# Where the first projections accumulate, and over how many bank tags the second piece's transposes rotate, in a hybrid decoder layer

## The chip, the cores and the metric

The kernel runs on one core of a Trainium2 chip. A core has five engines that run side by side, each through its own list of instructions in order: TensorE (PE, matrix products), VectorE (DVE), ScalarE (ACT), GpSimd (POOL) and SyncE (SP, which issues most of the transfers). PE writes its results only to PSUM, the accumulator memory, which this kernel uses as eight banks. The metric is the device time of one execution in microseconds; less is better. The result is given as the median of several runs, and as a ratio to runs of the kernel before on the same chip.

## The reference

One layer with 1024 tokens plus 16 learned ones ahead of them, 1024 wide:

```python
u = rmsnorm(h, g_pre_mix[l])
z = u @ w_in[l]
q, k, v, xr, yr = jnp.split(z, split_at, axis=-1)
attn = sliding_window_attention_with_sinks(q, k, v, attn_sinks[l])   # window 128
xr = causal_depthwise_conv(xr, conv_w[l], conv_b[l])
hr = rg_lru(xr, w_a[l], b_a[l], w_x[l], b_x[l], lru_lambda[l])
rec = gelu(yr) * hr
mix = jnp.concatenate([attn, rec], axis=-1) @ w_out[l]
h = h + rmsnorm(mix, g_post_mix[l])
u = rmsnorm(h, g_pre_ffn[l])
f = jnp.square(jax.nn.relu(u @ w_ff1[l])) @ w_ff2[l]
h = h + rmsnorm(f, g_post_ffn[l])
```

The change touches only the first two lines: the normed rows `u` and their projections.

## The kernel before

Every product of 32-bit numbers is made of three matmuls. An operand is split into a high part (a rounded copy, made by ACT) and a low part (the rest, made by DVE), and high by high, high by low and low by high are summed in PSUM (`mm3`, L122 to L128; `split`, L93).

The opening stage takes the 1040 rows in four pieces (`ALL`, L243): 272 rows (the 16 learned ones among them), then three times 256. For each piece, in `transposed` (L284), PE turns the normed rows by transposes (L291), eight chunks of 128 columns, each chunk in a bank of its own; ACT (L116) and DVE (L117) then scale each chunk and write the high and the low part of `u`, which empties the bank. After that come four projections with 128 columns each: k, v, the first q and the first x. Every projection of a piece is 24 matmuls (8 chunks by three parts) into one bank, and a sink empties it:

- `sink_k` (L359, `put_k` L352) is a ladder: for each of two halves ACT copies (L355), DVE copies (L356), DVE subtracts (L357). In the first piece it is done twice, once for the 16 learned rows and once for the other 256.
- `sink_v` (L372) and `sink_x` (L390) are one copy by ACT each.
- `sink_q` (L379) is an ACT step (L116) and a DVE step (L117) for each of two halves.

The first piece is written out apart (L403 to L418): k and v in two banks, then q, then x, each part by part (`part`, L234). The later pieces use `project` (L220), whose matmuls are L124 to L126. The norms of the later pieces (L209, L215) are made on ACT, POOL and DVE; those of the third and fourth piece run while the second piece is at work.

PSUM has four tags of two banks: acc, s, pt and o (`bank`, L65). A request for a bank of a tag gets whichever of its two banks comes free first. In the first piece all four projections ask for acc. The transposes go round over pt, o and s (L288), six banks. Later in the kernel s is the tag of the attention scores.

The order of the instructions on each engine isn't the order of the text. A planner simulates the kernel and at each moment gives an engine the instruction that is ready and stands earliest in the text; the order that comes out is fixed in the program. An instruction that has no bank in the planner's time is passed over by others that have one. Some orders are tied by hand: `behind` (L105), and `chained` (L271), which keeps ACT's and DVE's work of the opening in a row. The transposes of the third piece are tied behind the last matmul of the first piece, and so on (`done`, L396). The remaining projections (fills, L641) carry a lower priority and go between the steps of the attention, from about 64 us on.

Of the kernel before, what the change touches and what calls it, by code (L numbers as in the profile page):

```python
# [37 lines left out]
def hybrid_layer(  # L38
# [26 lines left out]
    def bank(tag, shape=(P, 512)):  # L65
        uid[0] += 1
        return ps.tile(list(shape), F32, tag=tag, name=f"ps_{tag}{uid[0]}")
# [37 lines left out]
    def behind(name, *inss):  # L105
        for ins in inss:
            tc.add_manual_dep(
                ins, name,
                mybir.DependencyInfo(
                    mybir.DependencyClass.NoSync, mybir.DependencyReason.DATA  # L110
                ),
                reason="order",
            )

    def split_scaled(hi, lo, src, scale):
        high = nc.scalar.activation(hi, src, AF.Copy, scale=scale).ins  # L116
        low = nc.vector.scalar_tensor_tensor(  # L117
            lo, src, scale, f32(hi), op0=ALU.mult, op1=ALU.subtract
        ).ins
        return high, low  # L120
# [99 lines left out]
    def project(w, pieces, sink):  # L220
        wh, wl = w
        for t0, n in pieces:
            acc = bank("acc")
            for kc in range(KC):
                uh, ul = u[kc]
                mm3(
                    acc[:, :n], (wh[:, kc, :], wl[:, kc, :]),
                    (uh[:, t0 : t0 + n], ul[:, t0 : t0 + n]),
                    kc == 0, kc == KC - 1,
                )  # L230
            sink(acc[:, :n], t0, n)


    def part(acc, w, piece, k, last=2):  # L234
        t0, n = piece
        for kc in range(KC):
            last_mm[0] = nc.tensor.matmul(
                acc[:, :n], w[k // 2][:, kc, :], u[kc][k % 2][:, t0 : t0 + n],
                start=k == 0 and kc == 0, stop=k == last and kc == KC - 1,
                skip_group_check=True,  # L240
            ).ins.name
# [19 lines left out]
    flip = [0]  # L261

    def normed(b):
        rows = [(meta_t, NMETA)] if b == 0 else []
        rows += [(xt[2 * b], P), (xt[2 * b + 1], P)]
        return [(norm_rows(s[:m], m), m) for s, m in rows]
# [4 lines left out]
    def chained(e, ins):  # L271
        if last[e] is not None:
            behind(last[e], ins)
        last[e] = ins.name
# [9 lines left out]
    def transposed(b, xn, after=None):  # L284
        t0, n = ALL[b]
        for kc in range(KC):
            flip[0] += 1
            pt = bank(("pt", "o", "s")[flip[0] % 3])  # L288
            o = 0
            for s, m in xn:  # L290
                ins = nc.tensor.transpose(  # L291
                    pt[:, o : o + m], s[:m, kc * P : (kc + 1) * P], ident[:m, :m]
                )
                if after:
                    behind(after, ins.ins)
                o += m
            uh, ul = u[kc]
            high = split_scaled(
                uh[:, t0 : t0 + n], ul[:, t0 : t0 + n], pt[:, :n],
                g_mix_col[:, kc : kc + 1],  # L300
            )
            if b == 0:
                chained(0, high[0])
                chained(1, high[1])
# [24 lines left out]
    for i in range(4, 8):  # L329
        load_x(i)  # L330
    wk = high_w(rk, "b")
    transposed(0, xn)
    low_w(wk, rk)
    wv = high_w(rv, "b")
# [64 lines left out]
    for b in range(4):  # L399
        if b:  # L400
            transposed(b, xn if b == 1 else normed(b), done[b])
        piece = ALL[b]
        if b == 0:  # L403

            acc = [bank("acc"), bank("acc")]
            for a, w in zip(acc, (wk, wv)):
                part(a, w, piece, 0)
                part(a, w, piece, 1)
            for a, w, sink in zip(acc, (wk, wv), (sink_k, sink_v)):
                part(a, w, piece, 2)  # L410
                sink(a[:, : piece[1]], *piece)
            for w, (t0, n), sink in ((wq, (16, 256), sink_q0), (wx, piece, sink_x0)):
                acc = bank("acc")
                for k in range(3):
                    part(acc, w, (t0, n), k)
                sink(acc[:, :n], t0, n)
            done.append(last_mm[0])
            continue  # L418
        project(wk, [piece], sink_k)
        project(wv, [piece], sink_v)  # L420
        project(wq, [piece], sink_q0)
        project(wx, [piece], sink_x0)
        done.append(last_mm[0])
# [64 lines left out]
    for b in range(2):  # L488
        pv = bank("pt", (P, 4, P))
        for i in range(4):  # L490
            o = NMETA + (4 * b + i) * P
# [852 lines left out]
```

## Time and profile before

| | us |
|---|---|
| median of 3 runs | 986.53 |
| lowest and highest run | 982.86, 989.44 |
| profiled execution, first to last instruction | 984.1 |

The time of the profiled execution is its span. Busy time is given for each engine; a matmul's row has its start and its length to the end of its result, and matmuls overlap, so that the pace is read from the starts. In rows that end with a bracket, the bracket gives the idle time of the engine before them, and what ended it. In a table by stretches each engine has its busy time and, in brackets, its number of instructions, in the order PE, weight loads (PEld), DVE, ACT, POOL; then come PE's granted clock as a share of full speed, the busy share of the DMA engines and GB/s. Tiles are named by tag: ps_acc is a bank of acc, a is `u`, ws and b are weights and sinks' targets.

### The profile page before, as it was taken

To read this page: it belongs to the slowest core of one execution; us is meant where nothing else is said; L and a number is where in the kernel's file an instruction comes from. 1 tells how busy PE (TensorE), PEld (TensorE's weight loads), DVE (VectorE), ACT (ScalarE), POOL (GpSimd) and SP (SyncE) were. 2 spreads that over 40 slices of the span, in tenths; PEclk is the share of its full clock that TensorE was granted. 3 is DMA by queue.
4 is the path that set the end of the run, shared out by engine and by line. 5 is a ranking of instruction groups with operands and counts; after the bars stand their busy time and mean duration, and the time that the engine had idled before them with its cause. 6 is when DMAs were issued, how large, how long until landed. Compare 5 with 4: busy or idle time off the path is not lost.

```text
span 984.1 us, 12519 instructions
## 1 busy us (share of the span) xinstructions
PE 955.5 (97%) x4782; PEld 803.2 (82%) x4782; DVE 680.7 (69%) x1002; ACT 502.3 (51%) x809; POOL 71.9 (7%) x108
## 2 busy tenths in 40 slices
PE   6799999999999999999999999999999999999995
PEld 6798999889878887888888888888888788888874
DVE  6469997775885687665655465468567776779876
ACT  7356665457944554343555556654433343435331
POOL 4010000000002100000000000000111000002012
PEclk9799999999999999999999999999999999999998
DMA  8002100112134466576522364324678766647762
GB/s 282 23 12 63 25 23 22 43 44 65 65 129 147 149 216 193 173 256 200 197 96 86 97 202 130 106 88 122 167 182 190 182 224 190 193 152 191 226 182 85
DMA packets 89371, 133.28 MB, mean 135 GB/s; under 512 B 13752, under 2 KB 52680, under 8 KB 89312
## 3 DMA queue, kind: packets, MB, share of 16 engines
q1 hardware_dynamic: 81488, 112.04, 35.9%
q0 software_dynamic: 6960, 18.35, 8.8%
q10 hardware_dynamic: 864, 2.10, 0.6%
q8 instruction: 37, 0.61, 0.3%
q14 instruction: 22, 0.18, 0.1%
HBM read 113.60 MB, written 18.87 MB: 135 GB/s over the span
## 4 chain that ended last, share of the span: by engine, by line
PE 87%; DVE 5%; DMA 4%; ACT 2%; issue 1%; POOL 1%; POOLq 0%; SPq 0%; DVEq 0%; ACTq 0%
PE ps_acc L125 10%; PE ps_acc L124 10%; PE ps_acc L126 10%; PE ps_s L126 6%; PE ps_s L124 6%; PE ps_s L125 6%; PE ps_pt L124 6%; PE ps_pt L126 6%; PE ps_pt L125 6%; PE ps_o L125 5%; PE ps_o L124 5%; PE ps_o L126 5%; DMA raw<-in_w_ff_dram 2%; PE ps_o L577 2%; PE ps_pt L566 1%
## 5 line engine op out<-in xcount | busy, mean ns | idle before, releaser
L95 ACT CAST ws<-raw 128x1024 fp32r<-128x1024 f32 (+1 forms) x70 | 71.7, 1025 | 124.9 <-PE ps_o L125 47.7
L98 DVE TENSOR_TENSOR ws<-raw,ws 128x1024 fp32r<-128x1024 f32 (+1 forms) x71 | 84.7, 1194 | 54.7 <-ACT ws L95 54.5
L124 PE MATMUL ps_acc<-a,ws 128*128 128x256 f32 (+2 forms) x256 | 85.8, 335 | 0.1
L125 PE MATMUL ps_acc<-a,ws 128*128 128x256 f32 (+2 forms) x256 | 85.3, 333 | 0.0
L126 PE MATMUL ps_acc<-a,ws 128*128 128x256 f32 (+2 forms) x256 | 84.9, 332 | 0.0
L98 DVE TENSOR_TENSOR b<-b,b 128x1024 fp32r<-128x1024 f32 (+2 forms) x48 | 57.6, 1201 | 26.1 <-PE ps_o L125 18.6
L95 ACT CAST ws<-e 128x1024 fp32r<-128x1024 f32 x42 | 43.8, 1043 | 57.6 <-PE ps_o L125 27.6
L95 ACT CAST b<-b 128x1024 fp32r<-128x1024 f32 (+2 forms) x48 | 49.4, 1030 | 43.5 <-DVE b L860 41.5
L98 DVE TENSOR_TENSOR ws<-e,ws 128x1024 fp32r<-128x1024 f32 x42 | 51.4, 1223 | 21.4 <-ACT ws L95 21.4
L126 PEld LDWEIGHTS ps_acc<-a,ws 128*128 128x128 f32 x256 | 48.2, 188 | 4.4
L124 PEld LDWEIGHTS ps_acc<-a,ws 128*128 128x128 f32 x256 | 48.3, 189 | 4.2 <-ACT c L391 0.3
L125 PEld LDWEIGHTS ps_acc<-a,ws 128*128 128x128 f32 x256 | 48.2, 188 | 3.7
L125 PE MATMUL ps_acc<-ws,b 128*128 128x512 f32 (+1 forms) x120 | 46.5, 388 | 1.1 <-DVE ws L98 1.1
L124 PE MATMUL ps_acc<-ws,b 128*128 128x512 f32 (+1 forms) x120 | 46.3, 386 | 0.9 <-ACT ws L95 0.9
L169 POOL TENSOR_TENSOR rs<-ms,half_pow 128x1 f32<-128x1 f32 (+1 forms) x31 | 21.7, 704 | 347.3 <-DVE ms L165 345.9
L126 PE MATMUL ps_acc<-ws,b 128*128 128x512 f32 (+1 forms) x120 | 46.2, 385 | 0.0
L124 PE MATMUL ps_pt<-ws,b 128*128 128x512 f32 x112 | 44.2, 395 | 0.0
L126 PE MATMUL ps_pt<-ws,b 128*128 128x512 f32 x112 | 44.1, 394 | 0.0
L125 PE MATMUL ps_pt<-ws,b 128*128 128x512 f32 x112 | 44.1, 394 | 0.0
L124 PE MATMUL ps_s<-ws,b 128*128 128x512 f32 x110 | 43.4, 394 | 0.0
L125 PE MATMUL ps_s<-ws,b 128*128 128x512 f32 x110 | 43.3, 394 | 0.0
L126 PE MATMUL ps_s<-ws,b 128*128 128x512 f32 x110 | 43.2, 393 | 0.0
(382 smaller groups left out, 2688.6 us busy)
## 6 DMA issues: line engine op xcount, KB each, us to landing
raw<-in_w_ff_dram SPq DMA_DIRECT2D x66, 512.0 KB, 3.9
e<-in_w_ff_dram SPq DMA_DIRECT2D x47, 512.0 KB, 3.7
d<-in_w_ff_dram SPq DMA_DIRECT2D x12, 512.0 KB, 3.9
s_dram<-d POOLq DMA_DIRECT2D x12, 512.0 KB, 3.8
raw<-in_w_in_dram SPq DMA_DIRECT2D x9, 512.0 KB, 3.9
raw<-in_w_ff_dram POOLq DMA_DIRECT2D x9, 512.0 KB, 7.2
c<-in_x_dram SPq DMA_DIRECT2D x8, 512.0 KB, 8.1
d<-in_x_dram SPq DMA_DIRECT2D x8, 512.0 KB, 5.0
```

Of the source, the lines that this page charges most:

```text
L95: nc.scalar.copy(hi, src)
L98: low = nc.vector.tensor_tensor(lo, src, f32(hi), op=ALU.subtract).ins
L124: nc.tensor.matmul(dst, lh, rh, start=start, stop=False, skip_group_check=True)
L125: nc.tensor.matmul(dst, lh, rl, start=False, stop=False, skip_group_check=True)
L126: last_mm[0] = nc.tensor.matmul(dst, ll, rh, start=False, stop=stop, skip_group_check=True).ins.name
L169: last_pow[0] = nc.gpsimd.tensor_tensor(rs[:n], ms[:n], half_pow[:n], op=ALU.pow).ins.name
L566: nc.tensor.transpose(pt[:, o : o + P], sn[h][:, 2 * bp + i, s * P : (s + 1) * P], ident,)
L577: nc.tensor.matmul(po[:, oc : oc + n], v, p_[:, pc : pc + n], start=first and k == 0, stop=last and k == 1, skip_group_check=True,)
```

## The change

q and x of the first piece ask for banks of s in place of acc. The second piece's transposes go round over pt and o alone; the other pieces' transposes still go round over three tags.

```diff
@@ transposed
         for kc in range(KC):
             flip[0] += 1
-            pt = bank(("pt", "o", "s")[flip[0] % 3])
+            pt = bank(("pt", "o", "s")[flip[0] % (2 if b == 1 else 3)])
@@ first piece
             for w, (t0, n), sink in ((wq, (16, 256), sink_q0), (wx, piece, sink_x0)):
-                acc = bank("acc")
+                acc = bank("s")
                 for k in range(3):
                     part(acc, w, (t0, n), k)
```

`flip` counts the chunks: 1 to 8 in the first piece, 9 to 16 in the second. With the remainder by 2 the second piece's chunks take o, pt, o, pt and so on, each tag four times. Nothing is computed otherwise than before, and the number of instructions stays.

## The prediction

> **What bounds the kernel now.** I read the page first, for the engine that is busy and where it is not.
>
> ```profile
> span 984.1 us, 12519 instructions
> ...
> PE 955.5 (97%) x4782; PEld 803.2 (82%) x4782; DVE 680.7 (69%) x1002; ACT 502.3 (51%) x809; POOL 71.9 (7%) x108
> ...
> PEclk9799999999999999999999999999999999999998
> ```
>
> TensorE (PE) is busy for 97% of the span. Slices are 24.6 us wide; the clock row falls below full only in the second slice and at the end, and the second slice is where the changed code runs. So I asked next for the waits of PE over the whole span, longest first (total us, times, longest).
>
> ```profile
> PE ps_o L153 <- DMA e<-in_g_pre_ffn_dram: 6.9, 1, 6.9
> PE ps_acc L237 <- DVE b L357: 5.6, 1, 5.6
> PE ps_acc L125 <- DVE ws L98: 1.1, 2, 0.8
> ```
>
> The first is the start, before any data. The second is one wait of 5.6 us: a projection matmul (L237) into an acc bank waits for L357, the last step of the k sink. Nothing later in the kernel costs PE more than 1.1 us. The timeline around that wait shows who stands where (start, length, engine, line).
>
> ```profile
> 13.32 6.22 PE L237 MATMUL ps_acc<-a,b 128*128 128x272 f32 x45
> 19.39 0.27 PE L291 MATMUL ps_pt<-ident,d 128*128 128x128 f32 x1
> ...
> 20.59 0.27 PE L291 MATMUL ps_s<-ident,d 128*128 128x128 f32 x1
> 20.62 3.09 PE L237 MATMUL ps_acc<-a,ws 128*128 128x256 f32 x24
> 24.23 0.44 PE L291 MATMUL ps_pt<-ident,d 128*128 128x128 f32 x2 [0.52 <-DVE a L117]
> 24.62 0.44 PE L291 MATMUL ps_o<-ident,d 128*128 128x128 f32 x2
> 30.62 5.81 PE L237 MATMUL ps_acc<-a,ws 128*128 128x272 f32 x24 [5.56 <-DVE b L357]
> 36.23 0.41 PE L124 MATMUL ps_acc<-a,b 128*128 128x256 f32 x1
> ...
> 36.78 0.28 PE L124 MATMUL ps_acc<-a,b 128*128 128x256 f32 x1
> ...
> 39.28 0.28 PE L124 MATMUL ps_acc<-a,b 128*128 128x256 f32 x1
> ```
>
> In order: k and v of the first piece, twelve transposes of the second piece, q (24 matmuls), four more transposes, the wait, x (24), then k of the second piece from 36.23 and, 24 rows later, its v from 39.28. Who holds the two acc banks is on the other engines:
>
> ```profile
> 20.12 0.38 ACT L373 COPY c<-ps_acc 128x272 f32<-128x272 f32 x1
> 30.14 0.43 DVE L357 TENSOR_TENSOR b<-ps_acc,b 64x256 fp32r<-64x256 f32 x1
> ```
>
> The v bank is emptied by one copy at 20.50, and q takes it. The k bank is emptied at 30.57, and x takes that one 0.05 us later. The k sink is a ladder of ACT and DVE steps in one bank, with other DVE work between its rungs. That is the wait. Its second price is the clock (PE busy; then the granted PE clock in the third value from the right):
>
> ```profile
> 27.00:28.00 1.00, 0.00 (x0) 0.00 (x0) 1.00 (x3) 0.86 (x3) 0.47 (x2) 0.50 0.05 13
> ...
> 35.00:36.00 1.00, 1.00 (x7) 1.00 (x5) 0.00 (x0) 0.00 (x0) 0.00 (x0) 0.50 0.00 0
> 36.00:37.00 1.00, 1.00 (x7) 1.00 (x7) 0.00 (x0) 0.39 (x1) 0.00 (x0) 0.68 0.00 0
> ```
>
> PE falls idle at 25.06 (24.62 + 0.44) and is at half clock from 27 to past 36, so all of x runs at half clock.
>
> **Part 1: q and x in score banks.** No instruction is added or removed; only banks, and with them the order that the planner writes out. The two s banks were last used by the first piece's transposes:
>
> ```profile
> 14.13 0.50 DVE L117 SCALAR_TENSOR_TENSOR a<-ps_s,gcol,a 128x272 fp32r<-128x272 f32 x1
> 22.20 1.22 DVE L282 TENSOR_TENSOR ws<-e,ws 128x1024 fp32r<-128x1024 f32 x1
> 23.70 0.47 DVE L117 SCALAR_TENSOR_TENSOR a<-ps_pt,gcol,a 128x256 fp32r<-128x256 f32 x1
> ...
> 24.88 0.47 DVE L117 SCALAR_TENSOR_TENSOR a<-ps_pt,gcol,a 128x256 fp32r<-128x256 f32 x1
> ...
> 27.01 0.48 DVE L117 SCALAR_TENSOR_TENSOR a<-ps_o,gcol,a 128x256 fp32r<-128x256 f32 x1
> 27.40 0.75 DVE L215 TENSOR_SCALAR d<-c,rs 128x1024 f32<-128x1024 f32 x1
> ```
>
> They are free at 14.63, before k and v end, so neither q nor x waits for a bank. The low half of the x weights (22.20, done 23.42) is needed only by the last third of x. Thus x can follow q at 23.71 (20.62 + 3.09). What this gives back, term by term, with the matmuls at the pace of the first row of the timeline (45 from 13.32 to 19.39: 0.135 us each):
> - the idle ahead of the four transposes: 0.52 us;
> - these transposes: 24.23 to 25.06 is 0.83, against 4 x 0.11 (12 took 19.39 to 20.62, 1.23 us, so some 0.10 to 0.11 each) = 0.44 in a stream: 0.39;
> - the wait itself: 5.56;
> - x at half clock: 36.23 - 30.62 = 5.61, against 24 x 0.135 = 3.24: 2.37;
> - the first three matmuls of the next k: 0.55 (36.23 to 36.78), against 3 x 0.118 (21 from 36.78 to 39.28, 2.50 us: 0.119 each) = 0.35: 0.20.
>
> The sum is 9.04 us. The v projection of the second piece, at 39.28 now, could start at 30.24.
>
> [...]
>
> **What is late next.** The second piece's k takes the old v bank, free since 20.50. Its v needs the old k bank, and that is free at 30.57 if ACT and DVE keep their order: 39.28 - 30.57 = 8.71, so 0.33 of the 9.04 goes to the new wait. Behind this v on PE stand the third piece's transposes, which begin with s banks, now held by q and x until their sinks are done:
>
> ```profile
> 31.46 0.43 DVE L117 SCALAR_TENSOR_TENSOR b<-ps_acc,b 64x256 fp32r<-64x256 f32 x1 [0.45 <-ACT b L116]
> ```
>
> That is q's last sink step, done at 31.89. The v projection would run to about 33.4 (30.57 + 24 x 0.119), so these transposes are covered by 1.5 us; if the sink came later than that, each us of it would count.
>
> **Part 2: four banks for the second piece's transposes.** Eight chunks of two transposes each go through pt and o alone. Chunks 5 to 8 wait for the eviction of 1 to 4, and whatever stands behind them on PE (x, or the next k) waits too. Before, six chunks went out at once and only two had to wait. The first four DVE evictions end at 25.35 (24.88 + 0.47), before x would end at 26.95; so, if the planner sets chunks 5 to 8 behind x, they cost no wait. If it sets them between q and x, x is held from 23.71 to 25.35: 1.64 us. There is a second place for the same loss. From 23.42 to 30.57 DVE has hardly a gap: eight of these evictions, three norms such as the 27.40 row, and the sink. Evictions 5 to 8 (4 x 0.39 = 1.6 us, the pitch between their starts) now come later, either ahead of the rest of the k sink, which moves v, or behind it, which moves k. The bounds are 0 and 1.6; no row decides between the two orders, and I take the middle, 0.8.
>
> Sum: 9.04 - 0.33 - 0.8 = 7.9 us. No DMA is moved; the weights of all four projections are split by 23.42.
>
> **Does it reach the end?** Each stage by PE busy of its length:
>
> ```profile
> 36.00:50.00 14.00, 14.00 (x119) 14.00 (x119) 4.97 (x12) 5.16 (x15) 0.00 (x0) 0.98 0.01 1
> 50.00:76.00 26.00, 26.00 (x224) 25.83 (x223) 17.45 (x58) 13.10 (x36) 2.71 (x4) 1.00 0.05 12
> 76.00:200.00 124.00, 123.37 (x854) 113.84 (x853) 107.37 (x281) 74.05 (x192) 0.00 (x0) 1.00 0.13 35
> ```
>
> PE has no gap from 36 to 76 and 0.63 us in the next 124, with DMA at 13% or less: nothing there is tied to a clock time, so all that is won at 39 moves everything behind it. The span would be 976.2. Three runs gave 982.86, 986.53 and 989.44, so the profiled execution, 984.1 from first to last instruction, lies among them; I take the difference off the median: 986.5 - 7.9 = 978.6. Their spread, 0.7%, is why I call under 1% no change.
>
> **The rivals.** *All of it comes back* (chance 0.18). The planner's order with free banks may put the k sink ahead of the norms; three norms at 0.75 are 2.25 us that it needn't wait for. Then neither the 0.33 nor the 0.8 is lost, and the time is 977.5. For it: the norms feed the third piece only. Against it: in the present order they stand ahead of the sink's rungs.
>
> *The wait moves to the four banks* (0.20). The planner sets chunks 5 to 8 ahead of x and DVE gets to the first four late. PE idles in short pieces that together last as long as what dropped the clock at 25 to 27. Price: 1.64 to 2 us of wait, and again about 2.6 of half clock (2.37 + 0.20): gain 9.04 - 0.33 - 2.0 - 2.6 = 4.1, time 982.4. For it: the 0.52 us wait on the same L117 with six banks. [...]
>
> *The attention stage is written out in a worse order, and it ends slower* (0.12). The planner times a new start and may draw the low-priority fill projections into other places. From 76 to 200 DVE is busy 107.37 of 124 us, and the fills are what keeps PE fed there. If a projection over all 1024 rows goes out too early, PE lacks it later: four pieces of 24 matmuls at 0.119, 11.4 us. The sum is then 7.9 - 11.4 = -3.5: 990.0. It turns the sign from 7.9 us of displaced fill on, two thirds of such a projection; two displaced ones would give 1001. For it: DVE's 87% in that stage. Against it: the stage begins on PE's progress, and all of it shifts together.
>
> *It doesn't do what it says, or is given back* (0.05): x still waits, for weights or for an order that keeps it behind the sink: 986.5.
>
> **The numbers.** The forecast, 978.6, keeps 0.45. Its own range by the bounds 0 and 1.6 and 2.5 us of run-to-run spread is 975 to 982. Below 975 the first rival and the spread leave about 0.1; above 987 lie about 0.1, most of them the third rival's. So 973 to 987. Faster by over 1% means under 976.7, a gain of 9.8: more than the 9.04 that this place holds, so it needs the spread or a better order later: 0.3 of the forecast, 0.6 of the first rival and a sixth of the second, together 0.28. Slower by over 1% is 996.4 and more: part of the third rival and what I haven't thought of, 0.07. The rest, 0.65, is within 1%.
>
> **What would show it.** Right: no PE wait on L357 of 5 us, clock 1.00 from 19 to 50, q and x rows named ps_s, the second piece's v starting between 30 and 32, and the same distance from there to the end. Four-bank rival: a PE wait on L117 of over 1.5 us between 22 and 28, clock below 1 behind it. Third rival: PE waits in 76 to 200 well above 0.6 us. I am wrong if v starts near 31 and the span has not shrunk by about as much.

## The result and the profile after

| | before | after |
|---|---|---|
| median of 7 runs, us | 986.22 | 979.06 |
| lowest and highest | 982.86, 989.44 | 973.93, 982.99 |
| profiled execution, span | 984.1 | 978.3 |

The ratio is 0.9921, 95% interval 0.9895 to 0.9948: faster by 0.8%, which is 7.8 us of 986.2; the two medians of the table lie 7.2 us apart. The forecast was 7.9. The waits of PE after, over the whole span:

```profile
PE ps_o L153 <- POOL ms L163: 6.7, 1, 6.7
PE ps_acc L124 <- ACT ws L95: 2.0, 1, 2.0
PE ps_acc L125 <- DVE ws L98: 0.8, 1, 0.8
...
PE ps_acc L124 <- DVE b L357: 0.2, 1, 0.2
```

The wait of 5.6 us on L357 is down to 0.2, and a wait of 2.0 us on ACT L95 has come up. The timeline of PE in the opening, after:

```profile
12.78 6.19 PE L237 MATMUL ps_acc<-a,b 128*128 128x272 f32 x45
18.81 0.27 PE L291 MATMUL ps_o<-ident,d 128*128 128x128 f32 x1
...
19.17 2.13 PE L237 MATMUL ps_s<-a,ws 128*128 128x256 f32 x16
21.14 0.27 PE L291 MATMUL ps_o<-ident,d 128*128 128x128 f32 x1
...
21.50 4.23 PE L237 MATMUL ps_s<-a,ws 128*128 128x256 f32 x32
25.56 0.38 PE L291 MATMUL ps_o<-ident,d 128*128 128x128 f32 x2
...
26.35 0.36 PE L124 MATMUL ps_acc<-a,b 128*128 128x256 f32 x1
...
33.73 0.36 PE L124 MATMUL ps_acc<-a,ws 128*128 128x256 f32 x1
```

q and x now write ps_s. The planner cut q in two, put half of the second piece's transposes before and between, and the other half behind x. The second piece's k starts at 26.35. The stages after:

```profile
19.00:26.00 7.00, 7.00 (x61) 7.00 (x60) 5.74 (x13) 3.78 (x11) 1.69 (x2) 1.00 0.86 257
26.00:36.00 10.00, 10.00 (x85) 9.73 (x84) 8.82 (x23) 8.11 (x21) 1.70 (x4) 1.00 0.06 15
36.00:50.00 14.00, 13.77 (x116) 13.45 (x116) 8.14 (x19) 7.29 (x18) 1.69 (x3) 1.00 0.08 19
50.00:76.00 26.00, 25.88 (x196) 24.40 (x196) 18.61 (x69) 12.59 (x36) 1.02 (x1) 1.00 0.17 42
76.00:200.00 124.00, 123.50 (x856) 114.11 (x855) 108.14 (x283) 74.58 (x192) 0.00 (x0) 1.00 0.11 31
```

PE has no gap from 19 to 36, and the clock stays at 1.00. To compare openings without the chance of the first transfers, I take the distance on PE from the second piece's first transpose, which follows k and v, to the first score matmul on keys. The rows of that matmul's line, before and then after (the last figures are the first and last start):

```profile
L518 PE MATMUL ps_s<-b,b x64: 272/281/367, 69.7 to 200.3; 128*128 128x256 f32 x56, 128*128 128x128 f32 x8
```

```profile
L518 PE MATMUL ps_s<-b,b x64: 271/282/368, 60.8 to 191.4; 128*128 128x256 f32 x56, 128*128 128x128 f32 x8
```

Before it is 69.7 - 19.4 = 50.3 us, after 60.8 - 18.8 = 42.0: 8.3 us less. The last score matmul of the line is as much earlier as the first (8.9 us, in which the start's 0.6 is contained), so the attention stage gave nothing back.

The lead lasts: the first of the last norms (L1183) starts at 838.9 before and 829.3 after, 9.6 us apart. The two profiled spans differ by only 5.8. The rest went in one place near the end. PE before and then after, around it:

```profile
938.10 0.51 PE L124 MATMUL ps_acc<-ws,b 128*128 128x512 f32 x1 [0.88 <-ACT ws L95]
939.36 0.50 PE L125 MATMUL ps_acc<-ws,b 128*128 128x512 f32 x1 [0.76 <-DVE ws L98]
939.70 0.39 PE L126 MATMUL ps_acc<-ws,b 128*128 128x512 f32 x1
939.93 0.39 PE L124 MATMUL ps_acc<-ws,b 128*128 128x512 f32 x1
```

```profile
929.65 0.49 PE L124 MATMUL ps_acc<-ws,b 128*128 128x512 f32 x1 [1.98 <-ACT ws L95]
930.91 0.79 PE L125 MATMUL ps_acc<-ws,b 128*128 128x512 f32 x1 [0.76 <-DVE ws L98]
931.50 0.63 PE L126 MATMUL ps_acc<-ws,b 128*128 128x512 f32 x1
931.93 0.63 PE L124 MATMUL ps_acc<-ws,b 128*128 128x512 f32 x1
```

The wait is 1.1 us longer, and behind it matmuls start every 0.43 us in place of 0.23: the clock has fallen to 0.50. By stretches of 1 us after, third value from the right:

```profile
930.00:931.00 1.00, 0.24 (x2) 0.09 (x1) 1.00 (x2) 0.55 (x1) 0.00 (x0) 0.65 0.00 0
931.00:932.00 1.00, 1.00 (x3) 0.81 (x4) 1.00 (x2) 0.00 (x0) 0.00 (x0) 0.50 0.02 8
...
937.00:938.00 1.00, 1.00 (x6) 0.82 (x5) 1.00 (x3) 0.14 (x1) 0.28 (x1) 0.94 0.87 96
```

What ACT waits for there is a weight load that GpSimd issued to add to a first one:

```profile
920.04 1.18 POOL L1121 DMA_DIRECT2D raw<-in_w_ff_dram  x1 [12.60 <-DMA raw<-in_w_ff_dram]
...
928.55 1.04 ACT L95 CAST ws<-raw 128x1024 fp32r<-128x1024 f32 x1 [6.47 <-DMA raw<-in_w_ff_dram]
```

The same two rows of a second trace of the changed kernel, in which PE has no wait there:

```profile
917.08 1.18 POOL L1121 DMA_DIRECT2D raw<-in_w_ff_dram  x1 [12.86 <-DMA raw<-in_w_ff_dram]
...
922.82 1.05 ACT L95 CAST ws<-raw 128x1024 fp32r<-128x1024 f32 x1 [2.11 <-DMA raw<-in_w_ff_dram]
```

So in the first trace this load was issued 3.0 us later and took 8.5 us in place of 5.7. GpSimd had waited for the load of the first summand, and the accumulating load ahead of this one was late by as much (906.23, against 903.01): the delay began with earlier transfers, and where, was not followed further.

### The profile page after: what moved, and what is told of

Read it like the earlier page. It is cut to its first block, busy times and chain, and to the rows that moved or that the text cites. A ratio compares the mean times of both kernels' runs of the same rounds, so it can differ in the third digit from the quotient of the medians.

```text
span 978.3 us, 12520 instructions
## 1 busy us (share of the span) xinstructions
PE 955.2 (98%) x4782; PEld 803.4 (82%) x4782; DVE 680.1 (70%) x1002; ACT 502.5 (51%) x809; POOL 71.3 (7%) x108
## 4 chain that ended last, share of the span: by engine, by line
PE 86%; DVE 4%; DMA 3%; issue 2%; ACT 2%; POOL 1%; POOLq 0%; DVEq 0%; SPq 0%; ACTq 0%
PE ps_acc L124 10%; PE ps_acc L125 10%; PE ps_acc L126 10%; PE ps_s L124 6%; PE ps_s L126 6%; PE ps_s L125 6%; PE ps_pt L124 6%; PE ps_pt L126 6%; PE ps_pt L125 6%; PE ps_o L124 5%; PE ps_o L125 5%; PE ps_o L126 5%; DMA raw<-in_w_ff_dram 3%; PE ps_o L577 2%; PE ps_pt L566 1%
## 5 line engine op out<-in xcount | busy, mean ns | idle before, releaser
L95 ACT CAST ws<-raw 128x1024 fp32r<-128x1024 f32 (+1 forms) x70 | 71.7, 1025 | 127.6 <-PE ps_o L125 43.4
L95 ACT CAST ws<-e 128x1024 fp32r<-128x1024 f32 x42 | 43.8, 1044 | 58.7 <-PE ps_o L125 25.9
L95 ACT CAST b<-b 128x1024 fp32r<-128x1024 f32 (+2 forms) x48 | 49.4, 1030 | 40.5 <-DVE b L860 38.5
```

What stands on the lines that cost most here:

```text
L95: nc.scalar.copy(hi, src)
```

## The experiments

The question was which part of the change carries the gain, whether the wait was the k bank and nothing else, and whether the loss near the end belongs to the change. All ratios are to the kernel before, with 95% intervals. Distances are those defined above.

**Only the banks.** Undone: the narrower rotation.

```diff
-            pt = bank(("pt", "o", "s")[flip[0] % (2 if b == 1 else 3)])
+            pt = bank(("pt", "o", "s")[flip[0] % 3])
```

> Only the banks: q and x of the first piece in s, the second piece's transposes still over three tags. Measure: the distance from the start of the row of 45 k and v matmuls to the first score matmul on keys, 56.4 us before (69.7 - 13.3) and 48.0 after (60.8 - 12.8). Bank theory (q and x waited only for the k bank, and s banks are to be had only if the transposes leave them alone): the 5.6 us wait on the k ladder is gone, but chunks 3 and 6 of the second piece now need the banks that q and x hold until their sinks, so k and v of that piece stop for 1 to 3 us: distance 49 to 51, time 980 to 983. Rival (the narrower rotation is a pure cost, six banks serve better than four): distance 48.0 or less, time 979 or less.

Measured: 0.9940 (0.9912 to 0.9968), median 980.97. From the first k and v row it is 63.0 - 13.4 = 49.6, inside what was expected, but that measure holds slow k and v matmuls here (the 45 took 7.29 us, against 6.19 after). From the first transpose it is 63.0 - 20.55 = 42.5, against 42.0. So the banks alone bring 7.8 of the 8.3 us of distance, and the contention for s costs some 0.5 us, not 1 to 3: the planner puts k and v matmuls of the second piece around the chunks that are late. In time this kernel can't be told from the full change.

**Only the rotation.** Undone: the banks (q and x back in acc).

```diff
-                acc = bank("s")
+                acc = bank("acc")
```

> Only the rotation: the second piece's transposes over two tags, q and x still in acc. Bank theory: x waits for the last step of the k ladder as before, about 5 us, with half clock behind it: distance 56 to 57.5 us, time 986 to 988. Rival (the gain came from the new order of the DVE work that the planner wrote out, with the norms behind the k ladder, and not from the banks): the ladder ends earlier here too, distance under 54, time 983 or less.

Measured: 1.0003 (0.9975 to 1.0031), median 987.30. The wait is there:

```profile
30.80 5.18 PE L237 MATMUL ps_acc<-a,ws 128*128 128x272 f32 x24 [4.82 <-DVE b L357]
35.82 0.27 PE L291 MATMUL ps_s<-ident,d 128*128 128x128 f32 x1
```

x starts at 30.80, at 30.62 before. The rival falls: the rotation alone brings nothing that the runs show. From the first k and v row the distance is 69.1 - 13.4 = 55.7, just below what was expected. From the first transpose it is 47.9, 2.4 less than before. k and v ran late in this trace (7.97 us for the 45) while the ladder did not, so that less of it was left to wait for (4.82 us); x takes 5.0 us and not 5.6; and the transposes behind q no longer wait 0.52 us for L117.

**The rotation alone, with the wait filled.** q and x are in acc, as in the kernel before, and 40 matmuls whose result nothing reads stand between them. The main part of the edit; other lines tie x's first matmul behind the last of the 40:

```diff
+                if w is wx:
+                    spare = bank("s")
+                    for i in range(N_IDLE):
+                        ins = nc.tensor.matmul(
+                            spare[:, :256], wq[0][:, i % KC, :], u[i % KC][0][:, 16:272],
+                            start=True, stop=True, skip_group_check=True,
+                        ).ins
+                        behind(last_mm[0], ins)
+                        last_mm[0] = ins.name
```

> As the rotation alone, with 40 matmuls added between q and x, whose result nothing reads: they fill the wait so that the clock has no reason to fall. Two-price theory (the wait cost 5.6 us of idleness and 2.6 of half clock): x still starts when the k ladder ends, but its 24 matmuls go at 0.135 us and not 0.234; distance 2.3 to 2.8 us shorter than with the rotation alone, time about 2.5 less. Rival (x is slow for another reason, its weights or its operands): 0.23 us each again and no difference over 0.5 us.

Measured: 0.9939 (0.9913 to 0.9965), median 980.98, a kernel with 40 needless matmuls that is 6.3 us faster than the same without them. PE in its opening:

```profile
22.99 4.92 PE L422 MATMUL ps_s<-a,ws 128*128 128x256 f32 x40
27.75 0.38 PE L296 MATMUL ps_o<-ident,d 128*128 128x128 f32 x2
...
28.43 3.25 PE L239 MATMUL ps_acc<-a,ws 128*128 128x272 f32 x24
31.52 0.27 PE L296 MATMUL ps_pt<-ident,d 128*128 128x128 f32 x1
```

x runs from 28.43 to 31.52, where the next row starts: 3.1 us, against 5.0 with the rotation alone (30.80 to 35.82) and 5.6 before. The granted clock reads 1.00 from 26 to 36 us here, 0.66 with the rotation alone and 0.52 before. So the clock's price is 1.9 to 2.5 us, where 2.3 to 2.8 was expected. The rest I had not expected: x no longer waits at all. The added matmuls hold chunks 5 to 8 back on PE, their evictions on DVE fall behind the k ladder, and the ladder's last step ends at 27.92:

```profile
27.49 0.43 DVE L362 TENSOR_TENSOR b<-ps_acc,b 64x256 fp32r<-64x256 f32 x1
```

(L362 is the ladder's last line in this kernel.) The end of the ladder isn't a fixed date; it depends on what DVE has between its rungs. The distance is 64.9 - 18.8 = 46.1, only 1.8 less than with the rotation alone, since the 40 matmuls take 4.8 us themselves. So the opening shows 1.8 of the 6.3 us, and only x's own pace can be put down to the clock. The other 4.5 lie outside this distance and were not traced to the 40 matmuls; start and end vary from run to run (the rotation alone had 983.0 to 991.9, this kernel 979.7 to 981.7).

**Only x in an s bank.** q stays in acc:

```diff
-                acc = bank("s")
+                acc = bank("s" if w is wx else "acc")
```

> The changed kernel, but of q and x only x goes to an s bank; q stays in acc. Measure: the distance from the first transpose of the second piece (the one that follows the k and v matmuls on PE) to the first score matmul on keys, which leaves the start of the kernel out: 50.3 us before (69.7 - 19.4), 42.0 after (60.8 - 18.8). Bank theory: q sits in the old v bank until its sink is done, so the second piece's k waits for the k ladder and its v for q's sink: distance 43.5 to 45, a PE wait of 1 to 2 us on L357 or L117, time 981 to 983. Rival (x's bank is all that matters): distance 42.0 within 0.4, time 979.

Measured: 0.9932 (0.9906 to 0.9959), median 978.29; distance 62.3 - 18.84 = 43.5. That is 1.5 us over the full change, the low edge of what was expected, but the waits are not those that were named: 0.7 us ahead of x, for the high part of its weights (ACT L278), because the planner put most of x ahead of q, and 0.4 on L357. In time it can't be told from the full change. x's bank carries most of the gain.

**Two banks in place of four.**

```diff
-            pt = bank(("pt", "o", "s")[flip[0] % (2 if b == 1 else 3)])
+            pt = bank("pt" if b == 1 else ("pt", "o", "s")[flip[0] % 3])
```

> The changed kernel with the second piece's transposes over one tag, two banks in place of four: each chunk from the third on waits for the eviction two before it. Rotation theory (PE waits for the return of the banks): distance, measured as for x alone, 44 to 46, with PE waits on L117 or L116 of over 1.5 us in total, time 981 to 983. Rival (the planner puts k and v matmuls of the second piece between the chunks, so fewer banks cost nothing): 42.0 to 42.6, time 979.

Measured: 0.9934 (0.9906 to 0.9962), median 980.70; distance 63.6 - 19.57 = 44.0, the low edge of the rotation theory. The PE waits of this stage, from 19 to 50 us:

```profile
PE ps_acc L124 <- DVE b L357: 0.8, 1, 0.8
PE ps_s L291 <- ACT c L391: 0.3, 1, 0.3
PE ps_acc L124 <- ACT a L116: 0.3, 1, 0.3
```

Halving the banks costs 2 us, 1.4 of it in these waits, and none on L117: it shows as matmuls of k that wait for a chunk (L116) and for a bank (L357). With four banks this price was below what the trace can show.

**The end.** Two more traces of the changed kernel and one of the kernel before:

> The changed kernel once more, for a second trace. Opening: distance 48.0 within 0.5 us. End: in its first trace PE waited 2.0 us for ACT L95 at 928 (before: 0.9 at 937), and the clock was at half for some 6 us after that. Chance theory (a weight transfer that GpSimd issues late lands by luck a little earlier or later): the wait lies anywhere from 0.5 to 2.5 us, and the clock falls only with the longest. Rival (the change moved that transfer for good): again 2.0 within 0.3 and the clock at half.

> A third trace of the changed kernel. Opening: distance 42.0 within 0.4 (42.0 and 41.9 so far). End: a wait on ACT L95 after 900 us and, where it is 2 us or more, half clock behind it; a trace without that wait has a span near 972, one with it near 978. If the span is 976 or more without such a wait and without a slice of lower clock, the spread between runs has another cause.

> The kernel before once more, for a second trace. Opening: the wait on the k ladder is there again, 4.5 to 6 us, and the distance from the second piece's first transpose to the first score matmul is 48 to 50.5 us (50.3 in the first trace, 47.9 with the rotation alone, which has the same wait). End: the PE wait on ACT L95 after 900 us anywhere from 0 to 3 us. If the distance were under 45 here, the opening would be a matter of luck and not of the banks.

| trace | distance, us | wait on L95 after 900 us | span, us |
|---|---|---|---|
| before | 50.3 | 0.9 | 984.1 |
| before, second | 50.2 | 1.6, then clock 0.93 from 925 to 950 | 985.0 |
| after | 42.0 | 2.0, then half clock | 978.3 |
| after, second | 41.9 | none | 972.1 |
| after, third | 41.8 | none | 972.9 |

The opening repeats within 0.2 us. The wait near the end doesn't: with the same program it comes and goes after the change, and is 0.9 or 1.6 us before it. First and second trace of the changed kernel have their last matmul at 967.06 and 960.92, 6.1 us apart, and at 829 us they are level (829.3 and 829.2 for the first L1183). The matmul behind the two waits starts at 930.91 in the first and 927.67 in the second, so the waits account for 3.2 of it; half clock from 930.3 to 937.1 accounts for the other 2.9. Thus the loss isn't the change's. Five traces do not tell whether the change made such a wait rarer.

**Against the spread.** First one weight sum of the last product was made by two plain loads and DVE:

```diff
-                q % 3 < 2 if i < 6 else q in (0, 2, 4)
+                q % 3 < 2 if i < 6 else q in (0, 2)
```

> The changed kernel with one weight sum late in the feed-forward stage (the fifth of its last seven products' eight steps) made by two plain loads and a DVE sum, in place of a load that GpSimd issues and that adds to what the first load brought. Tail theory: the PE wait on ACT L95 near 928 us (0.9 before, 2.0 in the first trace after, none in the second) comes from that late load and brings half clock with it when it is long; without it no PE wait over 0.5 us after 900 us, runs within 973 to 978 with a median near 974.5. Rival (another transfer is late in its place, or the sum delays DVE): the wait is there or greater, median 979 or more.

Measured: 0.9940 (0.9915 to 0.9965), median 981.73, runs from 975.6 to 982.3. Its trace has no wait after 900 us and a span of 974.2, but five of its eight runs lie at 981.6 and above, so the expectation fell: taking this load alone out doesn't narrow the spread. Then all three of these loads were taken out, and 20 transposes whose result nothing reads were put at the start, meant to have the clock up when the first data come:

```diff
     make_identity(nc, ident)
+    spare = bank("acc")
+    for i in range(20):
+        nc.tensor.transpose(spare[:, :P], ident, ident)
```

both together, and each alone.

> The changed kernel with two additions against the spread between runs: 20 transposes of the identity ahead of the first real one, whose result nothing reads, so that PE's clock is up when the first data come; and none of the last product's weight sums made by loads that GpSimd issues. Theory (the spread of some 8 us comes from the clock at the start and from the late load at the end): the first k and v matmuls at 0.135 us each from the start, no PE wait over 1 us after 900 us, runs within 4 us of one another, median 973 to 977. Rival (the spread has its cause elsewhere, or the plain loads are late too): runs spread over 6 us or more, median 978 or more.

> The changed kernel with only the first of the two additions: 20 transposes of the identity at the start, whose result nothing reads. The two additions together had runs of 976.2 to 978.7. Tail theory (the spread between runs comes from the late load and the half clock behind it): the spread stays, 973 to 982, and the clock over the span reaches down to 0.994. Start theory (it comes from the clock under the first matmuls): runs within 3 us of one another, 973 to 976.

> The changed kernel with only the second addition: no weight sum of the last product made by a load that GpSimd issues. Tail theory: runs within 4 us of one another, around 977, since the sums cost DVE some 2 us at the end (with both additions the last matmul was at 963.3 and the end 13.6 us later, against 11.2 in the changed kernel). Start theory: runs spread over 6 us or more.

| kernel | runs | lowest to highest, us | median | ratio (interval) |
|---|---|---|---|---|
| after | 7 | 973.9 to 983.0 | 979.06 | 0.9921 (0.9895 to 0.9948) |
| both additions | 6 | 976.2 to 978.7 | 977.42 | 0.9897 (0.9868 to 0.9926) |
| plain loads alone | 4 | 976.8 to 979.1 | 977.03 | 0.9899 (0.9871 to 0.9927) |
| early clock alone | 4 | 974.1 to 978.5 | 974.78 | 0.9884 (0.9847 to 0.9921) |

Both additions together kept the runs within 2.5 us, as expected, with a median 0.4 above the expected range. With the plain loads all ten runs lie within 3 us, and their lowest is 2 to 3 us above that of the changed kernel: from the last matmul to the end it is 13.6 us with both additions (963.28 to 976.9) and 13.7 with the plain loads alone (961.44 to 975.1), against 11.2 in the changed kernel. That speaks for the tail theory. The four runs of the early clock lie within 4.4 us, more than the start theory allowed and less than the tail theory foresaw; its own trace has no late wait, and the second piece's transposes start at 18.48, where the changed kernel's three traces have 18.57 to 19.14. The start does vary: with the rotation alone they start at 21.17, as PE did 27 matmuls from 12 to 18 us there and 44 to 46 in the three traces. The list of clock states in the kept traces begins with full clock at 18.0 with the rotation alone, at 11.3 to 12.2 in the three traces, and at 6.9 with the early clock (the stretches read 1.00 ahead of the first entry too). The two theories can't be told apart by these runs, nor can either kernel be told from the changed one: all intervals overlap.

## Why the prediction was right, and where it was not

**The wait and its two prices.** Right. From the first transpose to the first q matmul of the second piece the same work stands on PE in both kernels: 43.35 - 19.39 = 23.96 us before, 33.73 - 18.81 = 14.92 after. The row before:

```profile
43.35 0.36 PE L124 MATMUL ps_acc<-a,ws 128*128 128x256 f32 x1
```

The difference is 9.04 us, the sum that the prediction made of idleness, transposes and half clock. That it fits to the hundredth is luck: the further traces have 23.84 before and 14.83 and 14.65 after, so 8.9 to 9.3. The filled wait shows the clock's share by itself, 1.9 to 2.5 us for x.

**"0.33 to the new wait".** Wrong; there was no such loss. The bound was that ACT and DVE keep their order, with the k bank free at 30.57. They did not. The ladder's steps and the norms on DVE, after:

```profile
26.45 0.42 DVE L357 TENSOR_TENSOR b<-ps_acc,b 64x256 fp32r<-64x256 f32 x1
...
27.75 0.43 DVE L357 TENSOR_TENSOR b<-ps_acc,b 64x256 fp32r<-64x256 f32 x1
...
28.66 0.48 DVE L117 SCALAR_TENSOR_TENSOR a<-ps_o,gcol,a 128x256 fp32r<-128x256 f32 x1
...
31.07 0.75 DVE L215 TENSOR_SCALAR d<-c,rs 128x1024 f32<-128x1024 f32 x1
...
32.59 0.75 DVE L215 TENSOR_SCALAR d<-c,rs 128x1024 f32<-128x1024 f32 x1
```

The ladder ends at 28.18, 2.4 us earlier (1.8 if counted from the second piece's first transpose), with two norms behind it that stood ahead of its last rungs before, the row at 27.40 and this one:

```profile
28.95 0.73 DVE L215 TENSOR_SCALAR d<-c,rs 128x1024 f32<-128x1024 f32 x1
```

The prediction counted three norms there; the third (21.53) stands ahead of the ladder's first step on DVE (23.43). The evictions of chunks 5 to 8 went behind the ladder too (from 28.66). That is the mechanism of the first rival, to which I had given 0.18, with the evictions added.

**"I take the middle, 0.8", for the four banks.** Mis-sized: nothing by the time of the second q, as PE had no gap from 19 to 36. Two banks cost 2.0 us and six contested ones 0.5, so four is the right side of the range's end at 0.

**All that is won at 39 moves everything behind it.** Nearly. Of 9.04 us, 8.3 arrive at the first score matmul. PE stood still for 0.35 us between 36 and 76 (13.77 of 14, 25.88 of 26), where it had no gap before, 0.2 of it on L357; the other 0.4 was not followed further. From there to the first L1183 the lead stays: 9.6 us at 829, and 8.5 against the second trace before (837.8).

**The end** held a term that the prediction did not have: a late load, worth 6.1 us between two traces of the changed kernel. The forecast of 7.9 thus came out beside 7.8 (7.2 by the medians) with two losses charged that did not occur, 1.1 us together, and 0.7 us that was given back without being charged; that they nearly cancel is luck.

**The rivals.** The wait did not move to the four banks: no PE wait on L117 and clock 1.00 from 19 to 76. The prediction took the fall of the clock from the stretch at 27 (0.50), 1.9 us after PE stopped; the stretch before it (0.71) shows the fall already at 26.4, 1.4 us after PE stopped. The attention stage was not written out worse: PE 123.50 of 124, against 123.37.

## What to carry to other kernels

When a matmul waits for a bank, look at how long the sink that holds it takes and what else its engine does between the sink's steps; a product that follows needn't take that bank while another tag lies idle. Price such a wait with the clock behind it: here 5.6 us of idleness cost about 2 to 2.5 more. With a planner that writes the order anew, bounds taken from the old order of the other engines hold only as one case, and a distance between two fixed instructions on the busy engine tells more than the time of a run, when a late load at the end moves that by 6 us.

## What the runs showed of the hardware

With 40 needless matmuls ahead of x the granted clock read 1.00 from 26 to 36 us and x took 3.1 us; without them it read 0.66 (rotation alone) and 0.52 (before), and x took 5.0 and 5.6.

In these traces the length of a wait alone doesn't settle when the clock falls: in two traces of the kernel before it fell 1.4 and 4.0 us into a wait of 5.56. The packed traces before and after list only the clocks 1.00 and 0.50, so a stretch that reads between them dates the change; the fall in the opening before, and fall and return near the end of the second trace before:

```profile
26.00:27.00 1.00, 0.00 (x0) 0.00 (x0) 0.94 (x4) 1.00 (x4) 0.62 (x2) 0.71 0.69 204
...
940.00:941.00 1.00, 1.00 (x4) 0.78 (x4) 1.00 (x2) 0.17 (x1) 0.00 (x0) 0.61 0.88 227
...
943.00:944.00 1.00, 1.00 (x5) 0.81 (x4) 1.00 (x2) 0.00 (x0) 1.00 (x1) 0.68 0.75 268
```

| place | idleness of PE, us | half clock, us |
|---|---|---|
| opening before | 5.56, fall 1.4 after its start | 26.4 to 36.6: 10.2 |
| opening before, second trace | 5.56, fall 4.0 after its start | 28.9 to 35.7: 6.8 |
| opening, rotation alone | 4.82, fall 2.3 after its start | 28.2 to 35.1: 6.8 |
| end, after | 1.98 and 0.76 | 930.3 to 937.1: 6.8 |
| end before, second trace | 1.60 and 0.76 | 940.2 to 943.6: 3.4 |
| end, two banks | 2.85 and 0.77 | 935.9 to 939.3: 3.4 |
| end before | 0.88 and 0.76 | none |
| end, banks only | 1.2 and 0.8 | none |

The same wait of 5.56 us brought 10.2 us of half clock in one trace and 6.8 in the other, of which 6.0 and 5.3 lay under matmuls. The half clocks lasted 10.2, 6.8 or 3.4 us, the longer ones close to three and two times the shortest, and the falls in the opening came 1.4, 2.3 and 4.0 us after PE stopped, so that one figure for a single fall or return is not what these traces show.
